# A two-layer diffusion block on one core: modulation pages of four k-tiles, regrouped attention scores, an inverse masked where it is written, and part of the weight lows on GpSimd

## The chip, the core and the metric

The kernel runs on one core of a Trainium2 chip. TensorE multiplies matrices (it loads weights and streams columns; PE and PEld in the profile), VectorE (DVE), ScalarE (ACT) and GpSimd (POOL) do elementwise work, and SyncE (SP) issues the transfers. Every engine works through its own queue in order and waits for others by semaphores. The metric is the device time of one execution in microseconds; three runs of the kernel before took 1391.40, 1393.65 and 1397.22 us, and their median, 1393.65, is the time before.

## The reference

Two layers run over 256 context and 256 latent tokens of 1024 features. Cut to what matters here:

```python
mod = split(silu(c) @ ada_w[layer] + ada_b[layer], 6)        # shift, scale, gate, twice; also for the context
p = modulate(rms_norm(x), mod[0], mod[1]) @ w_in[layer]      # 30 tiles of 128 columns and 16 gate columns
# A: differential attention, 4 heads, two maps each
s = einsum(q, k) * 64 ** -0.5
w = softmax(s[map 0]) - lam * softmax(s[map 1])
o = w @ v
# B: HGRN2 gated recurrence.  C: gated DeltaNet, in chunks of 64:
tri = eye + where(strict, beta * (k @ k.T) * decay, 0)       # inverted for every chunk
u, w = solve(tri, [v * beta, k * beta * exp(gc)])
x = x + mod[2] * rms_norm(concat(A, B, C) @ w_out[layer])
x = x + mod[5] * rms_norm(conv_ffn(modulate(rms_norm(x), mod[3], mod[4])))
```

## The kernel before

The program holds the stream in transposed form, features on partitions and 512 tokens along the columns, and writes its stages as Python generators. `weave` steps several generators in turn at given rates (`RATE`, one row for each layer), which fixes the order in which the program is written; the framework's scheduler then orders the instructions of each engine from that order and the dependencies. The rates stand, in turn, for the projections of attention (`in_proj`), the gated DeltaNet (`gdn`), HGRN2 (`hgrn`), attention (`da`), the modulation (`ada`), and for the DeltaNet beside the late projections.

*Weights.* Each weight tile (`raw`, 128x1024) is split into a rounded part `whi` by ScalarE (L269) and the rest `wlo` by a subtraction (L273), and three matmuls for each k-tile add up the product. `wload` has a number `pool`: so many k-tiles of `wlo`, the last ones, are subtracted on GpSimd and the others on VectorE. In the output projection it is 2, in the attention projections (`proj_copy`) 0.

*Modulation.* `ada` computes one block of 512 columns from four pages of weights. A page holds two k-tiles; the matmul of a k-tile has 32 output rows and goes to one of four groups of array columns (`tile_position`), so a page uses two groups (L317). VectorE copies the result (`adas`, L320), four transposes turn it round (L323), and a reduction adds the four groups (L325). 12 blocks run inside the mixers and 8 in two fills beside the feed-forward part: six in layer 0 (about 400 to 515 us), two in layer 1 (about 1130 to 1190). Eight smaller units at the start (`ada_unit`, L337 and L343) already have four k-tiles to a page, and add the groups by a matmul with the constant `sel`.

*Attention.* For each head, stream and half of 128 queries, `da` makes two score matmuls (`sc`, L1035), one for each map, on different halves of the rows; each gets its maximum (`smx`, L1038), which VectorE multiplies by -0.125 (L1039), and an exponential (`em`, with the scale 0.125) that also sums the row (`ssm`). VectorE scales the first map (L1047) and adds the second (L1048); transposes (`wt`, L1052) and the product with `v` (`do`, L1060) follow.

*Gated DeltaNet.* `gdn` works in two halves of four chunks for two pairs of heads at a time (each list has a page for either pair). GpSimd multiplies the decays in page `gA` with beta (L658), VectorE multiplies them with the products `kk` into `N`, and six levels build the inverse in `MT` (page `gC`). At a level TensorE multiplies `N` with the inverse so far (`rt`), VectorE multiplies with a mask (L704), TensorE multiplies again (`dT`), and VectorE subtracts into `MT` (L707 at the first level, L721 after it). GpSimd also makes `gF` (L727, values times beta) and `gB` (L729, keys times decay), which are used after the inverse. In HGRN2 GpSimd updates `K` at each level (L930).

Of the kernel before, what the change touches and what calls it, by code (L numbers as in the profile page):

```python
# [43 lines left out]
)  # L44
RATE = ((121, 197, 32, 218, 37, 8), (53, 64, 15, 50, 5, 7))

GD_Q, GD_K, GD_V, GD_G = 0, 2, 4, 6
HG_Q, HG_G, HG_F, HG_I = 8, 10, 12, 16
DA_K, DA_V, DA_Q = 18, 22, 26
# [95 lines left out]
class Kernel:  # L145
# [161 lines left out]
    def ada(self, ly, blocks, tags=("raw",), bank="d"):  # L307
        nc = self.nc
        mod = self.mod[ly]
        for j in blocks:  # L310
            ps = self.bank(bank, "ada")
            for kc in range(4):
                w = self.load_raw(self.I["ada_w"][12 * ly + j - 4, kc], 1024, tags[kc % len(tags)]).rearrange("p (k n) -> p k n", k=2)
                for kk in range(2):
                    k = 2 * kc + kk
                    g = k % 4
                    nc.tensor.matmul(ps[32 * g:32 * g + 32, :], self.cs[:, k, :], w[:, kk, :], start=k < 4, stop=k >= 4,  # L317
                                     tile_position=(0, 32 * g))
# [171 lines left out]
    def evac(self, idx, dst, src):  # L490
        if idx % 2:
            self.nc.scalar.copy(dst, src)
        else:
            self.nc.vector.tensor_copy(dst, src)
# [53 lines left out]
    def gdn_gates(self, ly, ab):  # L548
# [48 lines left out]
        nc.vector.scalar_tensor_tensor(be, be, -1.0, beta, ALU.mult, ALU.mult)  # L597
        return dict(la=la, gc=gc, kd=kd, nbe=be, beta=beta)

# [4 lines left out]
    def gdn(self, ly, G, kq, v, last, res):  # L604
# [18 lines left out]
        for hf in range(2):  # L623
# [59 lines left out]
            for lev in range(LEVELS):  # L683
                b = 1 << lev

                def joint(t, c0, c1, bit0):
                    ap = t[:, 256 * bit0 + 64 * c0:256 * bit0 + 64 * c0 + 1]
                    return bass.AP(tensor=ap.tensor, offset=ap.offset,
                                   ap=[list(ap.ap[0]), [2 * b, (c1 - c0) * 32 // b], [b + (256 if bit0 == 0 else -256), 2], [1, b]])

                nb = lambda t: t.rearrange("p (n two b) -> p n two b", two=2, b=b)
                rt = [self.tmp("g2", "rt")[:, 0:256] for hp in HP]
# [18 lines left out]
                for g in range(2):  # L711
# [312 lines left out]
    def da(self, ly, h, q, k, vt, nl, gs, last, res):  # L1024
# [3 lines left out]
        for s, a, b in self.streams(lo):  # L1028
            nk = 2 if s == 0 else 4
            wts = []  # L1030
            for qt in range(2):
                e, rc = [], []
                for m in range(2):
                    ps = self.bank("a", "sc")
                    nc.tensor.matmul(ps[:, :128 * nk], q[64 * m:64 * m + 64, a + 128 * qt:a + 128 * qt + 128],  # L1035
                                     k[64 * m:64 * m + 64, :128 * nk], start=True, stop=True)
# [3 lines left out]
                    em = self.tmp("d2", "em")[:, :128 * nk]  # L1040
                    sm = self.small("sm", 1, 4)
                    self.act(em, ps[:, :128 * nk], AF.Exp, scale=0.125, bias=mx, accum_out=sm)
                    nc.vector.reciprocal(sm, sm)
                    e.append(em)
                    rc.append(sm)
                nc.vector.tensor_tensor(rc[1], rc[1], nl, ALU.mult)
                nc.vector.tensor_scalar(e[0], e[0], rc[0], None, ALU.mult)  # L1047
                nc.vector.scalar_tensor_tensor(e[0], e[1], rc[1], e[0], ALU.mult, ALU.add)  # L1048
                yield
                pt = self.bank("a", "wt")  # L1050
                for kk in range(nk):
                    nc.tensor.transpose(pt[:, 128 * kk:128 * kk + 128], e[0][:, 128 * kk:128 * kk + 128], self.C("ident"))  # L1052
# [313 lines left out]
def pack(inp):  # L1366
    f = lambda a: np.ascontiguousarray(np.asarray(a, dtype=np.float32))
    A = {}
# [15 lines left out]
    for gi, (f0, fn) in enumerate(GROUPS):  # L1384
        A[f"w_down{gi}"] = f(w[:, f0:f0 + fn].transpose(0, 3, 2, 1, 4)).reshape(DEPTH, KT, P, fn * P)
    w = f(inp["ada_w"]).reshape(DEPTH, 4, 2, P, 12, 512)
    A["ada_w"] = f(w.transpose(0, 4, 1, 3, 2, 5)).reshape(DEPTH * 12, 4, P, 1024)[4:]
    w = f(inp["ada_w"])[0].reshape(2, 4, P, 6, KT, P)[:, :, :, :2]
# [42 lines left out]
```

## Time and profile before

| what | us |
|---|---|
| median of three runs | 1393.65 |
| profiled execution, its own time | 1397.04 |
| its span, first to last instruction | 1395.3 |
| TensorE busy (10720 matmuls) | 1298.6 (93%) |
| VectorE busy (1722 instructions) | 892.5 (64%) |
| ScalarE busy (1189) | 658.9 (47%) |
| GpSimd busy (378) | 393.7 (28%) |

The profiled execution is one of its own, beside the three runs. Busy times are sums over the span, so stages with different limits lie in one number; the stages are told apart by stretches of time. In layer 0 the projections and gates end at about 145 us, the mixers at about 400, the output projection at about 455 and the feed-forward part at about 830; in layer 1 the mixers run to about 1145. TensorE's granted clock, 0.974 in the mean, is given for a stretch as a share of 2.4 GHz; 0.5 is the lower level.

### The profile page before, as it was taken

The page shows a single profiled execution, that of the slowest core. Times are in us where ns is not written, and L with a number is a line of the kernel's source. Part 1 is how long each engine was busy: PE and PEld are TensorE (multiplying, and loading weights), DVE is VectorE, ACT ScalarE, POOL GpSimd, SP SyncE. Part 2 cuts the span into 40 slices and gives each one's busy share as a digit, 9 for nine tenths or more (in the row PEclk, how much of TensorE's full clock was granted, in tenths as well). Part 3 has the DMA queues.
Part 4 walks back from the last instruction along what each step waited for, and adds up shares of the span by engine and source line. Part 5 has one row for each costly group of instructions (what it writes and reads, how often), then busy time and mean ns, then how long its engine had stood idle before and what let it go on. Part 6 is the DMA issues. An engine that isn't in the chain of part 4 may idle for free.

```text
span 1395.3 us, 26653 instructions
## 1 busy us (share of the span) xinstructions
PE 1298.6 (93%) x10720; PEld 1048.0 (75%) x10720; DVE 892.5 (64%) x1722; ACT 658.9 (47%) x1189; POOL 393.7 (28%) x378
## 2 busy tenths in 40 slices
PE   5999997999989999999999997999989998999996
PEld 2768665666677678888888886997666765999995
DVE  3565657877647876434543559877697665776665
ACT  3364424444465544323432455675253354655553
POOL 1012014201046223201210266221241024655553
PEclk8999998999999999999999999999999999999998
DMA  8612443112335663323233234544221265455552
GB/s 300 211 46 91 167 165 139 32 47 76 107 121 189 207 217 115 104 92 105 91 101 96 82 122 135 173 145 155 95 103 34 106 243 181 139 183 185 189 167 76
DMA packets 56283, 185.96 MB, mean 133 GB/s; under 512 B 6368, under 2 KB 10464, under 8 KB 56160
## 3 DMA queue, kind: packets, MB, share of 16 engines
q1 hardware_dynamic: 56160, 184.27, 39.9%
q8 instruction: 84, 1.38, 0.4%
q14 instruction: 39, 0.32, 0.1%
HBM read 182.14 MB, written 2.10 MB: 132 GB/s over the span
## 4 chain that ended last, share of the span: by engine, by line
PE 74%; DVE 12%; ACT 5%; POOL 4%; issue 2%; DMA 2%; SPq 0%; DVEq 0%; POOLq 0%; ACTq 0%
PE up L284 8%; PE up L283 8%; PE up L285 8%; PE in L293 6%; PE in L294 5%; PE in L295 5%; PE dn L285 4%; PE dn L284 4%; PE dn L283 4%; PE ada L317 2%; DVE wlo L273 2%; PE sc L1035 2%; PE op L284 1%; PE op L283 1%; PE op L285 1%
## 5 line engine op out<-in xcount | busy, mean ns | idle before, releaser
L273 DVE TENSOR_TENSOR wlo<-raw,whi 128x1024 fp32r<-128x1024 f32 (+2 forms) x241 | 299.8, 1245 | 269.1 <-issue 90.4
L269 ACT CAST whi<-raw 128x1024 fp32r<-128x1024 f32 (+1 forms) x244 | 248.9, 1023 | 122.6 <-PE dn L285 99.0
L285 PE MATMUL up<-h,whi 128*128 128x256 f32 (+1 forms) x768 | 248.7, 324 | 1.3 <-DVE h L441 0.7
L283 PE MATMUL up<-h,whi 128*128 128x256 f32 (+1 forms) x768 | 248.3, 324 | 1.2 <-ACT h L438 1.1
L284 PE MATMUL up<-h,wlo 128*128 128x256 f32 (+1 forms) x768 | 248.0, 324 | 0.9 <-DVE wlo L273 0.9
L293 PE MATMUL in<-h,whi 128*128 128x512 f32 (+1 forms) x496 | 184.8, 373 | 2.2 <-DVE kq L481 2.2
L273 POOL TENSOR_TENSOR wlo<-raw,whi 128x256 fp32r<-128x256 f32 (+1 forms) x111 | 127.1, 1145 | 173.2 <-ACT whi L269 76.4
L294 PE MATMUL in<-h,wlo 128*128 128x512 f32 (+1 forms) x496 | 175.5, 354 | 0.0
L295 PE MATMUL in<-h,whi 128*128 128x512 f32 (+1 forms) x496 | 175.3, 354 | 0.0
L283 PEld LDWEIGHTS up<-h,whi 128*128 128x128 f32 x768 | 145.8, 190 | 19.6 <-issue 4.2
L285 PEld LDWEIGHTS up<-h,whi 128*128 128x128 f32 x768 | 145.9, 190 | 16.4 <-issue 1.7
L284 PEld LDWEIGHTS up<-h,wlo 128*128 128x128 f32 x768 | 145.9, 190 | 15.5 <-DVE wlo L273 1.9
L284 PE MATMUL dn<-gT,wlo 128*128 128x256 f32 (+1 forms) x400 | 127.6, 320 | 3.4 <-DVE wlo L273 3.4
L283 PE MATMUL dn<-gT,whi 128*128 128x256 f32 (+1 forms) x400 | 127.7, 320 | 2.7 <-ACT gT L300 2.7
L285 PE MATMUL dn<-gT,whi 128*128 128x256 f32 (+1 forms) x400 | 127.3, 320 | 0.5 <-POOL gT L302 0.5
L1262 POOL TENSOR_TENSOR u<-u 128x512 f32<-128x512 f32 (+1 forms) x44 | 44.4, 1010 | 278.3 <-DVE u L481 257.5
L293 PEld LDWEIGHTS in<-h,whi 128*128 128x128 f32 x496 | 96.2, 194 | 19.8 <-issue 5.4
L294 PEld LDWEIGHTS in<-h,wlo 128*128 128x128 f32 x496 | 96.2, 194 | 12.7 <-issue 3.5
L295 PEld LDWEIGHTS in<-h,whi 128*128 128x128 f32 x496 | 95.9, 193 | 12.3 <-issue 1.3
L477 ACT ACTIVATE u<-up,vec 128x256 f32<-128x256 f32 (+1 forms) x96 | 61.8, 644 | 75.2 <-PE up L285 75.2
L284 PEld LDWEIGHTS dn<-gT,wlo 128*128 128x128 f32 x400 | 76.7, 192 | 9.1 <-DVE wlo L273 4.0
L283 PEld LDWEIGHTS dn<-gT,whi 128*128 128x128 f32 x400 | 76.8, 192 | 8.2 <-ACT gT L300 3.1
(281 smaller groups left out, 2318.2 us busy)
## 6 DMA issues: line engine op xcount, KB each, us to landing
raw<-ada_w SPq DMA_DIRECT2D x96, 512.0 KB, 4.4
raw<-w_up SPq DMA_DIRECT2D x96, 512.0 KB, 3.5
raw<-w_in SPq DMA_DIRECT2D x68, 512.0 KB, 3.6
raw<-w_down SPq DMA_DIRECT2D x32, 512.0 KB, 3.5
raw<-w_out SPq DMA_DIRECT2D x24, 512.0 KB, 3.5
raw<-w_down SPq DMA_DIRECT2D x24, 384.0 KB, 3.1
x<-xT SPq DMA_DIRECT2D x16, 256.0 KB, 6.1
x_spill<-x SPq DMA_DIRECT2D x8, 128.0 KB, 2.0
```

Source lines behind the costliest of these rows:

```text
L269: nc.scalar.copy(hi[:, :cols], raw[:, :cols])
L273: e.tensor_sub(lo[:, a:b], raw[:, a:b], hi[:, a:b].bitcast(F32))
L283: nc.tensor.matmul(ps, wh[:, k, :], ah, start=first and k == ks[0], stop=False)
L284: nc.tensor.matmul(ps, wl[:, k, :], ah, start=False, stop=False)
L285: nc.tensor.matmul(ps, wh[:, k, :], al, start=False, stop=last and k == ks[-1])
L293: nc.tensor.matmul(ps, wh[:, k, :], ah, start=k == 0, stop=False)
L294: nc.tensor.matmul(ps, wl[:, k, :], ah, start=False, stop=False)
L295: nc.tensor.matmul(ps, wh[:, k, :], al, start=False, stop=k == n - 1)
L317: nc.tensor.matmul(ps[32 * g:32 * g + 32, :], self.cs[:, k, :], w[:, kk, :], start=k < 4, stop=k >= 4, tile_position=(0, 32 * g))
L477: nc.scalar.activation(dst, ps, AF.Identity, scale=w3[1], bias=bias)
L1035: nc.tensor.matmul(ps[:, :128 * nk], q[64 * m:64 * m + 64, a + 128 * qt:a + 128 * qt + 128], k[64 * m:64 * m + 64, :128 * nk], start=True, ...
L1262: self.nc.gpsimd.tensor_mul(us[0][:, lo:], us[0][:, lo:], us[1][:, lo:])
```

## The change

`ada` takes four k-tiles of 256 columns from a page, so that each page uses all four groups, and adds the groups by four matmuls with `sel` in place of transposes and reduction; the weights are packed in that order. In `da` both score matmuls of a query half are written next to each other, the second map's first; the maximum is negated in its own instruction, the scale 0.125 moves to the copy of the query projection (ScalarE), the scaling of the first map moves from VectorE to ScalarE, and lambda goes in by a `tensor_scalar`. In `gdn` the sign moves into beta (`nb`), `rt` is no longer masked but copied by ScalarE, and the new `fill` writes only the masked places of `MT` by `copy_predicated`. `proj_copy` gives two k-tiles of the lows to GpSimd. Four of six rates change in each layer.

```diff
-RATE = ((121, 197, 32, 218, 37, 8), (53, 64, 15, 50, 5, 7))
+RATE = ((121, 179, 35, 218, 38, 8), (47, 64, 10, 62, 5, 6))
...
-            for kc in range(4):
-                w = self.load_raw(self.I["ada_w"][12 * ly + j - 4, kc], 1024, tags[kc % len(tags)]).rearrange("p (k n) -> p k n", k=2)
-                for kk in range(2):
-                    k = 2 * kc + kk
-                    g = k % 4
-                    nc.tensor.matmul(ps[32 * g:32 * g + 32, :], self.cs[:, k, :], w[:, kk, :], start=k < 4, stop=k >= 4,
-                                     tile_position=(0, 32 * g))
+            prev = []
+            for i in range(4):
+                half, kc = i // 2, i % 2
+                w = self.load_raw(self.I["ada_w"][12 * ly + j - 4, i], 1024, tags[i % len(tags)]).rearrange("p (k n) -> p k n", k=4)
+                for g in range(4):
+                    x = nc.tensor.matmul(ps[32 * g:32 * g + 32, 256 * half:256 * half + 256], self.cs[:, 4 * kc + g, :], w[:, g, :],
+                                         start=kc == 0, stop=kc == 1, tile_position=(0, 32 * g))
+                    prev = [self._dep(x, prev)]
...
-                nc.tensor.transpose(ps2[:, 128 * i:128 * i + 128], st[:, i * 128:(i + 1) * 128], self.C("ident"))
-            sm = self.small("adr", 8)
-            nc.vector.reduce_sum(sm, ps2.rearrange("p (a g s) -> p a s g", a=4, g=4)[:, :, 0:2, :], axis=AX.X)
+                nc.tensor.matmul(ps2[:, 2 * i:2 * i + 2], st[:, 128 * i:128 * i + 128], self.C("sel"), start=True, stop=True)
...
-        w = self.wload(self.I["w_in"][ly, idx], 8, 128)
+        w = self.wload(self.I["w_in"][ly, idx], 8, 128, 2)
...
-        self.evac(idx, dst[:, lo:], ps[:, lo:])
+        self.evac(idx, dst[:, lo:], ps[:, lo:], 0.125 if idx >= DA_Q else None)
...
-                nc.gpsimd.tensor_tensor(ck(X[hp]), ck(X[hp]), b64(hp, "beta"), ALU.mult)
+                nc.gpsimd.tensor_tensor(ck(X[hp]), ck(X[hp]), b64(hp, "nb"), ALU.mult)
...
+                def fill(t, src):
...
+                    nc.vector.copy_predicated(out, m.bitcast(U32), v(src))
...
-                for hp in HP:
-                    nc.vector.tensor_tensor(ck(rt[hp]), ck(src[hp]), hgm[:, lev, :].unsqueeze(1).to_broadcast([P, 4, 64]), ALU.mult)
                 if lev == 0:
                     for hp in HP:
-                        nc.vector.tensor_tensor(joint(MT[hp], 0, 4, 0), joint(MT[hp], 0, 4, 0), nb(rt[hp]), ALU.subtract)
+                        fill(MT[hp], src[hp])
                     yield
                     continue
+                for hp in HP:
+                    nc.scalar.copy(rt[hp], src[hp])
...
-                    nc.vector.tensor_tensor(joint(MT[hp], 0, 4, 0), joint(MT[hp], 0, 4, 0), nb(ps2[hp][:, 0:256]), ALU.subtract)
+                    fill(MT[hp], ps2[hp][:, 0:256])
...
-                    mx = self.small("mx", 1, 4)
-                    nc.vector.reduce_max(mx, ps[:, :128 * nk], axis=AX.X)
-                    nc.vector.tensor_scalar(mx, mx, -0.125, None, ALU.mult)
...
-                    self.act(em, ps[:, :128 * nk], AF.Exp, scale=0.125, bias=mx, accum_out=sm)
...
-                nc.vector.tensor_scalar(e[0], e[0], rc[0], None, ALU.mult)
...
+                    for n, t in enumerate(qs):
+                        for m in (1, 0):
+                            x = nc.tensor.matmul(ps[m][:, 128 * nk * n:128 * nk * n + 128 * nk],
...
+                            prev.append(self._dep(x, prev[-1:]))
...
+                        nc.vector.reduce_max(mx[m][:, :len(qs)], ps[m][:, :128 * nk], axis=AX.X, negate=True)
...
+                nc.scalar.activation(e0, e0, AF.Copy, scale=r0)
+                nc.vector.reciprocal(r1, r1)
+                nc.vector.tensor_scalar(r1, r1, nl, None, ALU.mult)
+                nc.vector.scalar_tensor_tensor(e0, e1, r1, e0, ALU.mult, ALU.add)
```

The first place is GpSimd's queue in layer 0, where the DeltaNet's second half begins, in the kernel before (`sgl` is a small copy, `gA_1983` and `gA_1984` are the pages of the two pairs of heads, `sbeta` is beta, `skd` the decays):

```order
L678 COPY sgl_2153<-gB_1986 128x8
L658 TENSOR_TENSOR gA_1983<-gA_1983,sbeta_640 128x512
L727 TENSOR_TENSOR gF_2725<-gB_1985,sbeta_640 128x512
L729 TENSOR_TENSOR gB_1985<-gB_1985,skd_676 128x256
L727 TENSOR_TENSOR gF_2725<-gB_1986,sbeta_640 128x512
L729 TENSOR_TENSOR gB_1985<-gB_1985,skd_676 128x256
L729 TENSOR_TENSOR gB_1986<-gB_1986,skd_676 128x256 x2
L658 TENSOR_TENSOR gA_1984<-gA_1984,sbeta_640 128x512
L930 TENSOR_TENSOR K_203_1175<-K_203_1175,F_202_1174 128x128x2x2 x2
```

The same place in the changed kernel (`snbt` is beta with the sign turned, `wlo` with L273 is a weight tile's lows):

```order
L681 COPY sgl_2309<-gB_2072 128x8
L661 TENSOR_TENSOR gA_2069<-gA_2069,snbt_683 128x512
L661 TENSOR_TENSOR gA_2070<-gA_2070,snbt_683 128x512
L738 TENSOR_TENSOR gF_2868<-gB_2071,sbeta_640 128x512
L740 TENSOR_TENSOR gB_2071<-gB_2071,skd_676 128x256 x2
L273 TENSOR_TENSOR wlo_2338<-raw_2335,whi_2337 128x256
L738 TENSOR_TENSOR gF_2868<-gB_2072,sbeta_640 128x512
L740 TENSOR_TENSOR gB_2072<-gB_2072,skd_676 128x256 x2
L273 TENSOR_TENSOR wlo_2605<-raw_2602,whi_2604 128x256
```

The second `gA` page's multiplication moved from behind all of `gF` and `gB` to right behind the first, and the lows of weight tiles stand between the two pairs' `gF` and `gB` and behind them.

The second place is the same one in layer 1, in the kernel before:

```order
L678 COPY sgl_10110<-gB_9932 128x8
L658 TENSOR_TENSOR gA_9929<-gA_9929,sbeta_8652 128x512
L727 TENSOR_TENSOR gF_10684<-gB_9931,sbeta_8652 128x512
L658 TENSOR_TENSOR gA_9930<-gA_9930,sbeta_8652 128x512
L729 TENSOR_TENSOR gB_9931<-gB_9931,skd_8688 128x256 x2
L727 TENSOR_TENSOR gF_10684<-gB_9932,sbeta_8652 128x512
L729 TENSOR_TENSOR gB_9932<-gB_9932,skd_8688 128x256 x2
```

And in the changed kernel:

```order
L681 COPY sgl_10182<-gB_9981 128x8
L661 TENSOR_TENSOR gA_9978<-gA_9978,snbt_8747 128x512
L738 TENSOR_TENSOR gF_10635<-gB_9980,sbeta_8704 128x512
L740 TENSOR_TENSOR gB_9980<-gB_9980,skd_8740 128x256 x2
L661 TENSOR_TENSOR gA_9979<-gA_9979,snbt_8747 128x512
L738 TENSOR_TENSOR gF_10635<-gB_9981,sbeta_8704 128x512
L740 TENSOR_TENSOR gB_9981<-gB_9981,skd_8740 128x256 x2
```

Here the second `gA` page's multiplication moved the other way, past the two `gB` multiplications of the first pair.

## Rows read from the trace of the kernel before

**Rows 1.** Stretches: length, busy of PE, PEld, DVE, ACT, POOL (count), clock, DMA.
```profile
215.00:400.00 185.00, 164.06 (x1918) 115.83 (x1916) 130.68 (x343) 86.11 (x216) 39.19 (x37) 0.93 0.21 70
445.00:515.00 70.00, 65.13 (x426) 46.12 (x425) 53.87 (x98) 34.78 (x62) 17.19 (x18) 1.00 0.65 218
985.00:1145.00 160.00, 147.12 (x1823) 104.28 (x1821) 121.48 (x330) 70.81 (x159) 35.86 (x31) 0.97 0.33 117
```

**Rows 2.** Waits of TensorE, 215 to 400: who for whom, sum us, times, longest.
```profile
PE rt L602 <- DVE gC L707: 8.3, 1, 8.3
PE wt L1052 <- DVE em L1048: 5.0, 6, 1.3
```

**Rows 3.** GpSimd in order of time, 213 to 231: start, us, instruction.
```profile
214.56 1.05 POOL L658 TENSOR_TENSOR gA<-gA,sbeta 128x512 f32<-128x512 f32 x1 [2.13 <-ACT gA L222]
215.56 3.70 POOL L727 TENSOR_TENSOR gF<-gB,sbeta 128x512 f32<-128x512 f32 x1
219.34 2.63 POOL L729 TENSOR_TENSOR gB<-gB,skd 128x256 f32<-128x256 f32 x1
...
225.75 1.04 POOL L658 TENSOR_TENSOR gA<-gA,sbeta 128x512 f32<-128x512 f32 x1
226.75 3.18 POOL L930 TENSOR_TENSOR K<-K,F 128x512 f32<-128x512 f32 x2
```

**Rows 4.** ScalarE, VectorE and TensorE in order of time around the 8.3 us.
```profile
217.55 0.63 ACT L222 ACTIVATE gA<-gA 128x512 f32<-128x512 f32 x1
...
226.82 1.72 DVE L668 TENSOR_TENSOR gA<-gA 128x256 f32<-128x256 f32 x1 [3.18 <-POOL gA L658]
...
233.47 0.87 PE L602 MATMUL rt<-gC,gA 64*64 64x64 f32 x10 [8.32 <-DVE gC L707]
```

**Rows 5.** Short stretches behind the stall and in layer 1, columns as above.
```profile
226.00:236.00 10.00, 2.53 (x35) 2.00 (x35) 7.67 (x21) 4.54 (x11) 3.85 (x3) 0.70 0.29 107
236.00:246.00 10.00, 10.00 (x111) 7.01 (x109) 6.88 (x23) 5.29 (x12) 0.00 (x0) 0.62 0.18 54
...
1030.00:1040.00 10.00, 7.22 (x118) 4.93 (x119) 10.00 (x24) 4.50 (x11) 5.86 (x6) 0.95 0.38 141
```

**Rows 6.** The modulation's products (L317) alone, by stretch.
```profile
145.00:215.00 70.00, 9.62 (x80) 2.09 (x80) 1.00 0.53 188
445.00:515.00 70.00, 19.02 (x72) 2.67 (x72) 1.00 0.65 218
```

**Rows 7.** The start's products and weight loads of `sel`; weight loads of the transposes.
```profile
40.38 0.64 PE L337 MATMUL ada<-raw,cs 128*32 128x256 f32 x8
...
48.08 0.62 PEld L343 LDWEIGHTS ada<-consts,adas 128*128 128x128 f32 x4
...
484.76 0.46 PEld L323 LDWEIGHTS ada<-consts,adas 128*128 128x128 f32 x4
```

**Rows 8.** Score matmuls in order of time: one alone, a pair side by side.
```profile
247.48 1.12 PE L1035 MATMUL sc<-qk 64*128 64x512 f32 x2
...
295.80 1.13 PE L1035 MATMUL sc<-qk 64*128 64x512 f32 x4
```

**Rows 9.** Durations by line: busy us, mean ns, idle; last two 215 to 400.
```profile
L704 DVE TENSOR_TENSOR rt<-rt,consts 128x256 f32<-128x256 f32 x40 | 15.1, 410 | 6.2 <-PE rt L602 6.2
...
L917 DVE COPY_PREDICATED Stot<-consts,hs 128x512 f32<-128x512 uint32 x12 | 8.1, 730 | 1.6 <-PE hs L892 1.6
...
L1047 DVE TENSOR_SCALAR em<-em,ssm 128x256 f32<-128x256 f32 (+1 forms) x16 | 6.6, 413 | 0.2
...
L1039 DVE TENSOR_SCALAR smx<-smx 128x1 f32<-128x1 f32 x32 | 4.6, 145 | 0.4
```

**Rows 10.** A weight tile's lows on both engines, output projection, in order of time.
```profile
408.17 0.96 DVE L273 TENSOR_TENSOR wlo<-raw,whi 128x768 fp32r<-128x768 f32 x1 [1.92 <-PE op L285]
408.20 1.53 POOL L273 TENSOR_TENSOR wlo<-raw,whi 128x256 fp32r<-128x256 f32 x1 [0.65 <-PE op L285]
409.04 0.97 DVE L404 TENSOR_TENSOR acc<-acc,sq 128x256 f32<-128x256 f32 x1
```

More of the change, by code (lines that the diff above doesn't have):

```diff
@@ L483, in proj_copy, with evac @@
     def proj_copy(self, ly, idx, hT, lo, dst):
-        w = self.wload(self.I["w_in"][ly, idx], 8, 128)
+        w = self.wload(self.I["w_in"][ly, idx], 8, 128, 2)
         ps = self.bank("d", "in")
         yield from self.dense_gen(ps[:, lo:], w, hT, lo, NTOK)
-        self.evac(idx, dst[:, lo:], ps[:, lo:])
+        self.evac(idx, dst[:, lo:], ps[:, lo:], 0.125 if idx >= DA_Q else None)
         yield
-    def evac(self, idx, dst, src):
-        if idx % 2:
+    def evac(self, idx, dst, src, scale=None):
+        if scale is not None:
+            self.nc.scalar.activation(dst, src, AF.Copy, scale=scale)
+        elif idx % 2:
             self.nc.scalar.copy(dst, src)
@@ L597, in gdn_gates @@
         nc.vector.scalar_tensor_tensor(be, be, -1.0, beta, ALU.mult, ALU.mult)
-        return dict(la=la, gc=gc, kd=kd, nbe=be, beta=beta)
+        nbeta = self.small("nbt", 32, 1)
+        nc.vector.tensor_scalar(nbeta, beta, -1.0, None, ALU.mult)
+        return dict(nb=nbeta, la=la, gc=gc, kd=kd, nbe=be, beta=beta)
     def quad(self, items):
@@ L689, in joint @@
                                    ap=[list(ap.ap[0]), [2 * b, (c1 - c0) * 32 // b], [b + (256 if bit0 == 0 else -256), 2], [1, b]])
+                def fill(t, src):
+                    ap = t[:, 0:1]
+                    out = bass.AP(tensor=ap.tensor, offset=ap.offset,
+                                  ap=[list(ap.ap[0]), [64, 4], [2 * b, 32 // b], [b + 256, 2], [1, b]])
+                    v = lambda t: t.rearrange("p (c n two b) -> p c n two b", c=4, two=2, b=b)
+                    m = hgm[:, lev, :].rearrange("p (n two b) -> p n two b", two=2, b=b).unsqueeze(1).to_broadcast([P, 4, 32 // b, 2, b])
+                    nc.vector.copy_predicated(out, m.bitcast(U32), v(src))
                 nb = lambda t: t.rearrange("p (n two b) -> p n two b", two=2, b=b)
@@ L1031, in da @@
             for qt in range(2):
[L1032 to L1036, printed above, removed]
-                    mx = self.small("mx", 1, 4)
-                    nc.vector.reduce_max(mx, ps[:, :128 * nk], axis=AX.X)
-                    nc.vector.tensor_scalar(mx, mx, -0.125, None, ALU.mult)
-                    em = self.tmp("d2", "em")[:, :128 * nk]
-                    sm = self.small("sm", 1, 4)
-                    self.act(em, ps[:, :128 * nk], AF.Exp, scale=0.125, bias=mx, accum_out=sm)
-                    nc.vector.reciprocal(sm, sm)
-                    e.append(em)
-                    rc.append(sm)
@@ L1046, in da @@
-                nc.vector.tensor_tensor(rc[1], rc[1], nl, ALU.mult)
-                nc.vector.tensor_scalar(e[0], e[0], rc[0], None, ALU.mult)
-                nc.vector.scalar_tensor_tensor(e[0], e[1], rc[1], e[0], ALU.mult, ALU.add)
+                if True:
+                    qs = (qt,)
+                    ps = [self.bank("a", "sc") for m in range(2)]
+                    prev = []
+                    for n, t in enumerate(qs):
+                        for m in (1, 0):
+                            x = nc.tensor.matmul(ps[m][:, 128 * nk * n:128 * nk * n + 128 * nk],
+                                                 q[64 * m:64 * m + 64, a + 128 * t:a + 128 * t + 128],
+                                                 k[64 * m:64 * m + 64, :128 * nk], start=True, stop=True)
+                            prev.append(self._dep(x, prev[-1:]))
+                    mx = [self.small("mx", 2, 4) for m in range(2)]
+                    es = {}
+                    for m in range(2):
+                        nc.vector.reduce_max(mx[m][:, :len(qs)], ps[m][:, :128 * nk], axis=AX.X, negate=True)
+                        for n, t in enumerate(qs):
+                            em = self.tmp("d2", "em")[:, :128 * nk]
+                            sm = self.small("sm", 1, 8)
+                            self.act(em, ps[m][:, 128 * nk * n:128 * nk * n + 128 * nk], AF.Exp, bias=mx[m][:, n:n + 1], accum_out=sm)
+                            es[t, m] = em, sm
@@ L1049, in da @@
+                (e0, r0), (e1, r1) = es[qt, 0], es[qt, 1]
+                nc.vector.reciprocal(r0, r0)
+                nc.scalar.activation(e0, e0, AF.Copy, scale=r0)
+                nc.vector.reciprocal(r1, r1)
+                nc.vector.tensor_scalar(r1, r1, nl, None, ALU.mult)
+                nc.vector.scalar_tensor_tensor(e0, e1, r1, e0, ALU.mult, ALU.add)
                 yield
@@ L1051, in da @@
                 for kk in range(nk):
-                    nc.tensor.transpose(pt[:, 128 * kk:128 * kk + 128], e[0][:, 128 * kk:128 * kk + 128], self.C("ident"))
+                    nc.tensor.transpose(pt[:, 128 * kk:128 * kk + 128], e0[:, 128 * kk:128 * kk + 128], self.C("ident"))
                 wt = self.tmp("r2", "wt")
@@ L1385, in pack @@
         A[f"w_down{gi}"] = f(w[:, f0:f0 + fn].transpose(0, 3, 2, 1, 4)).reshape(DEPTH, KT, P, fn * P)
-    w = f(inp["ada_w"]).reshape(DEPTH, 4, 2, P, 12, 512)
-    A["ada_w"] = f(w.transpose(0, 4, 1, 3, 2, 5)).reshape(DEPTH * 12, 4, P, 1024)[4:]
+    w = f(inp["ada_w"]).reshape(DEPTH, 2, 4, P, 12, 2, 256)
+    A["ada_w"] = f(w.transpose(0, 4, 5, 1, 3, 2, 6)).reshape(DEPTH * 12, 4, P, 1024)[4:]
     w = f(inp["ada_w"])[0].reshape(2, 4, P, 6, KT, P)[:, :, :, :2]
```

2 lines of the change are left out of this document (1 added, 1 removed).

## The prediction

> **What bounds the kernel now.** I read four views in this order: busy time by stretch, TensorE's waits, the order of time around the longest wait, and durations by line. The stretches [rows 1] show a kernel that lives on TensorE: even in the two mixer stretches (215 to 400 us in layer 0, 985 to 1145 in layer 1) it is busy 164.06 of 185 and 147.12 of 160 us. So only two things can shorten the run: less work on TensorE, or less of its idle time, which is 20.9 us in the first stretch and 12.9 in the second. The waits [rows 2] name what is in the first: one wait of 8.3 us (`rt` on VectorE's `gC`, L707) and six of 5.0 us in sum (`wt` on `em`, L1048). The order of time shows what lies behind the 8.3 us: GpSimd [rows 3] multiplies the first `gA` page at 214.56, then takes six multiplications for `gF` and `gB`, and comes to the second `gA` only at 225.75, although ScalarE had that page's exponential done at 218.2 [rows 4]. VectorE sits 3.18 us for it, needs until 234 for the inverse's first level, and TensorE starts `rt` at 233.47. Then the clock pays again [rows 5]: in 226 to 236 the granted clock is 0.70, in 236 to 246 it is 0.62, so of these 20 us some 6.0 and 7.6 are at the 1.2 GHz level.
>
> The sum is made against the profiled execution's own 1397.04 us (span 1395.3, 1.7 around it), which is 3.4 us above the median of 1393.65; at the end I take 3.4 off.
>
> **A. Modulation pages.** Four pages per block stay four, with transfers of the same number and size; each now brings four k-tiles of 256 columns instead of two of 512. Where pages come one by one, a page costs TensorE 19.02 / 18 = 1.06 us today (72 records, four a page, 445 to 515) [rows 6]; the new form exists in the kernel's start (L337) and takes 0.64 us a page [rows 7]. There are 32 such pages in the two fills; I count 24 as coming alone: 24 x 0.42 = -10 us. Where all four pages wait ready (12 blocks inside the mixers) a block costs 9.62 / 5 = 1.92 us today and between that and 4 x 0.64 = 2.56 in the new form; the columns streamed are the same, so I stay near today's row with 2.1, +2 us. The second step gets dearer: four transposes load weights for 0.46 us, while the form with `sel` loads for 0.62 us per two products, since an fp32 product passes twice [rows 7]. Four products are 1.24 at most, so +0.78 a block at most and, as runs follow each other closely, I take +0.65; 20 blocks, +13 us, 8 of them in the mixers and 5 in the fills. On the path: the mixers get +10 of work, of which TensorE's idle slots hide a little, +9. The fills get 5 less, but there the elementwise chain of the norms sets much of the pace (TensorE is busy 65.13 of 70), so -3. A is +6, bounds -3 (the fills' 5 whole and a little more, the mixers' part hidden) and +17 (2.56 and 0.78 a block in the mixers, nothing from the fills).
>
> **B. Scores.** Two score matmuls of one head use different halves of the rows, and a pair side by side takes 1.13 us where one alone takes 1.12 [rows 8]. But 19 of the 24 pairs stand side by side in TensorE's queue already, and in the changed order it is 17. The pairing does not do what its name says; what is left is that the first one issued now waits for the bank that comes free last, so that staggered pairs close up. -1, bounds -4 and +3.
>
> **C. GpSimd's queue in layer 0.** The rates move the gated delta net against the rest, and the second `gA` multiplication now stands right behind the first, ahead of all of `gF` and `gB`. Its page is ready at 218.2, so it could end at 219.3 instead of 226.8: 7.5 us. TensorE has about the same work between `kk` and `rt` as before, a little less, so I take 6.5 of the 8.3. The slow clock behind the stall costs half of what TensorE did at 1.2 GHz (some 2 and 7.6 us): -4.5. C is -11, bounds 0 and -13.
>
> **D. VectorE gets lighter.** Gone are 48 mask products (0.41 each, 19.7 us) and 24 scalings of `e0` (0.413 mean, 9.9 us); the 48 tiny multiplications by -0.125 (0.145 each) overlap their neighbours, I count half, 3.5 us [rows 9]. `copy_predicated` takes the place of a subtraction of the same size: 0.73 us at 512 columns, so about 0.41 at 256; nothing. That is 33 us, about a tenth of VectorE's load in the mixers (130.68 and 121.48 us in the two stretches [rows 1], the rest ahead of them); 20 small sums of the modulation and four copies of `q` go too, uncounted. Where it is full and TensorE waits (10.00 of 10 us at 1030 to 1040, TensorE at 7.22 [rows 5]) a tenth comes back directly. The idle time left after C is 20.9 + 12.9 - 8.3 = 25.5 us; a third of it, -8, with the clock that goes with it. Against it: the scaling of `e0` moves behind the second exponential on ScalarE, one hop more in 24 chains that end in `wt`; behind a scaling that waits stand ScalarE's casts of the next weights, which are a tile ahead of TensorE. At 0.4 to 0.5 us each that is +12 at worst; the negated maximum saves a hop in the same chains, so I take +1. The 40 copies of `rt` that ScalarE takes over stand in the place of VectorE's products in the same chain; ScalarE is busy 86 of 185 and 71 of 160 us [rows 1], and they hide. D is -7, bounds -25 and +12.
>
> **E. Lows on GpSimd.** 28 weight tiles give their last two k-tiles to GpSimd, VectorE's part shrinks by a quarter. In the output projection, which does it today, the pair reads [rows 10]: VectorE 0.96 us from 408.17, GpSimd 1.53 us from 408.20, so it ends at 409.73, and the next VectorE instruction, a 128x256 sum, takes 0.97. GpSimd first waits for VectorE's part and then VectorE for GpSimd's. The long L668 beside GpSimd's `K` (1.72 us from 226.82) [rows 3, 4] is the same. Per tile VectorE saves at most 0.96 x 256 / 768 = 0.32 us, and loses at most 0.97 - 0.41 = 0.56 (a sum of that size takes 0.41 undisturbed, as L704 does [rows 9]): -9 to +7 over 28 tiles, and I take 0. TensorE uses the two k-tiles last, so GpSimd has most of a tile's time for them; nothing is added there.
>
> The Trainium skill, "SBUF — State Buffer", section "Who interferes with whom", says that VectorE with two SBUF inputs and GpSimd reading SBUF exclude each other for a whole instruction, which speaks against E. The 0.97 us row agrees. If every low on GpSimd locked VectorE for its own 0.57 us (1.53 - 0.96) it would be 28 x 0.57 = 16 us on VectorE's side, half of what D takes off it, and the run would be some 4 us longer than forecast.
>
> **F. GpSimd in layer 1.** Here the new order puts the second `gA` behind one `gF` and two `gB`; before, only behind one `gF`. +1, upper bound 13 (a stall like the one in layer 0, 8.3 + 4.5).
>
> **Sum.** 6 - 1 - 11 - 7 + 0 + 1 = -12, so 1385 in the profiled execution's terms and, less 3.4, 1381 on the scale of the median.
>
> **Rivals.** *Nothing gained:* the relief of VectorE does not reach TensorE because its queue is in order and the next wait ends last, and C brings half (-5): 6 - 1 - 5 + 0 + 1 = +1, some 1395. For it: beside the 8.3 us the idle time is in waits of one or two microseconds, of which each can be replaced by another. Against it: VectorE really is full where TensorE waits. *More gained:* the idle time left falls by 70% (-18, so D is -17) and A's fill part comes through whole (A is +4): 4 - 1 - 11 - 17 + 0 + 1 = -24, about 1370. For it: where VectorE is full, TensorE waits for nothing else. Against it: only 30 to 40 us of the mixers look like that. *Slower: the stall moves to layer 1.* The second `gA` of layer 1 waits behind `gF` and both `gB`; at layer 0's durations (3.70 and 2.63 us with VectorE beside them [rows 3]) that is over 7 us, and as in layer 0 the chain to `rt` behind it takes 6.7 more (226.8 to 233.5) while TensorE has a few microseconds of projection. Price 8.3 + 4.5 = +13, and with VectorE held by GpSimd there, D falls to -1; with A's mixer part whole and nothing from the fills (+10): 10 - 1 - 11 - 1 + 0 + 13 = +10, about 1404. It decides when that second multiplication starts more than 5 us after the first. Against it: it is the shorter queue of the two, three instructions against six in layer 0 today.
>
> **Chances.** Forecast 0.50 (its own range 1375 to 1389), more gained 0.14, nothing gained 0.20, slower 0.16. A measurement of this kernel tells about 0.5% (7 us) from no change. Below 1386.7 lie nine tenths of the forecast and all of "more": 0.60; the rest of the forecast, "nothing" and a little of "slower" (0.02): 0.26; slower 0.14. The range of 8 in 10 reaches from 1366, below "more", to 1400, past "nothing gained" and short of "slower".
>
> **What would show it.** C right: no wait of `rt` over 3 us in layer 0's second half of the delta net, clock 1.00 behind it. A right: the modulation's products in 445 to 515 fall to about 12 us, the second step rises from 0.46 to about 1.1 us of weight loads a block. B right: score pairs at 1.13 us, but no fewer separate ones. D right: VectorE's busy time falls by some 35 us, and TensorE's idle time in the mixers by 15 to 20. E right: 28 more GpSimd lows of over 1 us, and VectorE's parts near 1 us. The prediction is wrong if the wait in C is still there or comes up in layer 1, or if waits of `in` for lows on GpSimd appear.

## The result: slower by 0.8%, outside the range

The changed kernel took 1406.47 us in the median (1400.82 to 1413.38, 12 runs), the kernel before 1395.83 beside it; the ratio is 1.0075 with an interval of 1.0054 to 1.0095. The forecast was 1381, the range ended at 1400. The profiled execution, 1400.94 us with a span of 1399.2, is one of the shortest of the twelve, so the profile shows only some 4 of the 10.6 us. The rest goes with the clock: the mean granted clock of the twelve runs goes from 0.974 (1400.94 us) down to 0.962 (1413.38 us), with a median of 0.969, while the runs of the kernel before beside the experiments have medians of 0.977 to 0.979.

### The profile page after: what moved, and what is told of

The parts are those of the page before. It is cut to its first block, busy times and chain, and to the rows that moved or that the text cites. A ratio compares the mean times of both kernels' runs of the same rounds, so it can differ in the third digit from the quotient of the medians.

```text
span 1399.2 us, 27455 instructions
## 1 busy us (share of the span) xinstructions
PE 1307.8 (93%) x11120; PEld 1071.9 (77%) x11120; DVE 869.0 (62%) x1580; ACT 682.6 (49%) x1257; POOL 421.5 (30%) x406
## 4 chain that ended last, share of the span: by engine, by line
PE 53%; DVE 9%; ACT 2%; issue 1%; POOL 1%; DMA 1%; DVEq 0%; POOLq 0%; ACTq 0%
PE up L284 8%; PE up L285 8%; PE up L283 8%; PE dn L285 4%; PE dn L284 4%; PE dn L283 4%; PE in L293 3%; PE in L295 2%; PE in L294 2%; DVE wlo L273 2%; PE ada L317 1%; DVE x L467 1%; PE ada L324 1%; PE ss L382 1%; PE sc L1049 1%
## 5 line engine op out<-in xcount | busy, mean ns | idle before, releaser
L273 DVE TENSOR_TENSOR wlo<-raw,whi 128x768 fp32r<-128x768 f32 (+2 forms) x241 | 296.4, 1231 | 263.4 <-PE up L284 91.2
L273 POOL TENSOR_TENSOR wlo<-raw,whi 128x256 fp32r<-128x256 f32 (+1 forms) x139 | 153.3, 1106 | 277.2 <-ACT whi L269 128.4
L1281 POOL TENSOR_TENSOR u<-u 128x512 f32<-128x512 f32 (+1 forms) x44 | 49.0, 1114 | 284.9 <-DVE u L480 284.9
```

What stands on the lines that cost most here:

```text
L273: e.tensor_sub(lo[:, a:b], raw[:, a:b], hi[:, a:b].bitcast(F32))
L1281: self.nc.gpsimd.tensor_mul(us[0][:, lo:], us[0][:, lo:], us[1][:, lo:])
```

## The profile after

The stretches of [rows 1], now (length, busy of PE, PEld, DVE, ACT, POOL, clock, DMA):

```profile
215.00:400.00 185.00, 176.04 (x2010) 128.91 (x2009) 122.12 (x285) 107.64 (x265) 47.46 (x52) 0.98 0.26 82
445.00:515.00 70.00, 64.94 (x528) 55.23 (x527) 49.94 (x83) 34.24 (x57) 16.59 (x17) 0.93 0.66 217
985.00:1145.00 160.00, 143.91 (x1764) 103.55 (x1763) 112.05 (x271) 72.24 (x165) 42.28 (x39) 0.94 0.33 112
```

Layer 0 went the way of the forecast: TensorE is busy for 176.04 of 185 us instead of 164.06, VectorE's time falls from 130.68 to 122.12. The third row goes the other way: TensorE's idle time there is 16.1 us where it was 12.9, at a clock of 0.94, although VectorE has 9.4 us less to do. In the second row the clock, 1.00 before, is 0.93.

TensorE's longest waits between 215 and 400, in answer to [rows 2], then GpSimd around the second half of the DeltaNet, in layer 0 and in layer 1, in answer to [rows 3]:

```profile
PE wt L1071 <- DVE em L1067: 3.5, 4, 1.7
PE sc L1049 <- DVE rope L1031: 1.3, 1, 1.3
```

```profile
219.21 2.14 POOL L661 TENSOR_TENSOR gA<-gA,snbt 128x512 f32<-128x512 f32 x2
226.07 1.04 POOL L738 TENSOR_TENSOR gF<-gB,sbeta 128x512 f32<-128x512 f32 x1 [4.73 <-ACT gB L545]
...
1014.22 1.04 POOL L661 TENSOR_TENSOR gA<-gA,snbt 128x512 f32<-128x512 f32 x1 [1.06 <-ACT gA L222]
1015.22 1.22 POOL L738 TENSOR_TENSOR gF<-gB,sbeta 128x512 f32<-128x512 f32 x1
1016.52 1.43 POOL L740 TENSOR_TENSOR gB<-gB,skd 128x256 f32<-128x256 f32 x2
1019.31 1.09 POOL L661 TENSOR_TENSOR gA<-gA,snbt 128x512 f32<-128x512 f32 x1 [1.36 <-ACT gA L222]
```

The 8.3 us wait is gone, and in layer 0 both `gA` pages are multiplied one right behind the other. In layer 1 the second page starts 5.1 us after the first, just past the point that the rival set; yet the longest wait of `rt` there is 2.1 us, and the next rows tell where the time is instead. They are two stretches of layer 1: from the first `rt` to the last (the DeltaNet's inverses), and from there to the first `up` matmul (the tail: late projections, HGRN and attention, the output projection, two modulation blocks). The kernel before:

```profile
950.30:1069.50 119.20, 108.05 (x1357) 76.61 (x1360) 95.02 (x228) 54.30 (x113) 28.98 (x24) 0.96 0.30 102
1069.50:1179.30 109.80, 102.66 (x1172) 76.57 (x1162) 68.71 (x183) 52.32 (x115) 26.73 (x24) 1.00 0.46 159
```

The changed kernel:

```profile
945.10:1061.00 115.90, 101.10 (x1295) 73.66 (x1291) 84.95 (x172) 56.09 (x124) 34.28 (x29) 0.94 0.29 96
1061.00:1188.60 127.60, 120.25 (x1358) 89.49 (x1348) 73.95 (x185) 59.63 (x132) 34.48 (x32) 0.96 0.43 150
```

The inverses gain 3.3 us, the tail loses 17.8. TensorE's idle time in the tail is 7.1 us before and 7.4 now: what grew there is its busy time, at a clock of 0.96 for 1.00. HGRN's products `hs` tell what moved: here in the changed kernel, and behind it in experiment e1, where layer 1 has its old rates (count, durations in ns, first and last start):

```profile
L903 PE MATMUL hs<-Q,kj x192: 218/218/284, 1017.0 to 1118.9; 64*64 64x64 f32 x192
```

```profile
L903 PE MATMUL hs<-Q,kj x192: 218/218/366, 986.6 to 1069.2; 64*64 64x64 f32 x192
```

## The experiments

Ratios are to the kernel before on the same chip; an interval is about 0.002 to either side, so the difference of two ratios is good to some 0.003, 4 us. "New" and "old" order are the rates of a layer as in the changed kernel and as before.

| run | order L0, L1 | work | us | ratio (interval) |
|---|---|---|---|---|
| changed | new, new | all new | 1406.47 | 1.0075 (1.0054, 1.0095) |
| e1 | new, old | all new | 1387.87 | 0.9953 (0.9930, 0.9975) |
| e5 | old, old | all new | 1401.44 | 1.0057 (1.0038, 1.0075) |
| e6 | old, new | old | 1414.07 | 1.0134 (1.0106, 1.0162) |
| e11 | new, old | old | 1387.99 | 0.9961 (0.9946, 0.9976) |
| e9 | new, HGRN 10 | all new | 1398.35 | 1.0035 (1.0016, 1.0054) |
| e10 | new, attention 62 | all new | 1388.97 | 0.9972 (0.9954, 0.9989) |
| e16 | new, HGRN 20 | all new | 1398.66 | 1.0022 (1.0003, 1.0041) |
| e2 | new, new | old modulation | 1404.50 | 1.0054 (1.0033, 1.0075) |
| e3 | new, new | old DeltaNet | 1397.75 | 1.0005 (0.9984, 1.0027) |
| e4 | new, new | old lows | 1404.20 | 1.0063 (1.0039, 1.0087) |
| e7 | new, old | old DeltaNet | 1388.86 | 0.9950 (0.9936, 0.9965) |
| e8 | new, old | old modulation | 1387.61 | 0.9952 (0.9935, 0.9968) |
| e12 | new, old | old attention | 1400.16 | 1.0053 (1.0040, 1.0066) |
| e13 | new, old | old lows | 1389.52 | 0.9954 (0.9934, 0.9975) |
| e14 | new, old | new attention alone | 1385.00 | 0.9920 (0.9899, 0.9941) |
| e15 | new, old | new lows alone | 1396.43 | 1.0012 (0.9997, 1.0027) |
| e17 | new, old | e14 and pages, transposes | 1385.68 | 0.9931 (0.9907, 0.9955) |
| e18 | new, old | e14 and new modulation | 1385.20 | 0.9931 (0.9906, 0.9956) |

### The order of layer 1: e1, e6, e9, e10, e16

```diff
 e1:  -(47, 64, 10, 62, 5, 6)   +(53, 64, 15, 50, 5, 7)   on the changed kernel
 e6:  -(53, 64, 15, 50, 5, 7)   +(47, 64, 10, 62, 5, 6)   on the kernel before
 e9:  e1 with (53, 64, 10, 50, 5, 7)
 e10: e1 with (53, 64, 15, 62, 5, 7)
 e16: e1 with (53, 64, 20, 50, 5, 7)
```

> The changed kernel with the four rates of layer 1 put back to (53, 64, 15, 50, 5, 7); layer 0 keeps the new rates. In the changed kernel the stretch from the first rt of layer 1 to the feed-forward part there is 14.5 us longer (950.3 to 1179.3 before, 945.1 to 1188.6 after), while layer 0 up to the feed-forward part is 8.7 us shorter. Theory 1 (the order of layer 1, set by its rates, is what costs): the time falls by 8 to 14 us against the changed kernel, to 1392 to 1398, at or a little under the kernel before. Theory 2 (the work that changed, modulation or DeltaNet, is what costs, wherever it stands): it falls by under 3 us, to 1403 to 1406.

> The kernel before with only the rates of layer 1 changed to (47, 64, 10, 62, 5, 6). Theory 1 (the order itself is what costs): slower than the kernel before by 10 to 19 us, 1406 to 1415. Theory 2 (the order costs only together with the new DeltaNet or modulation work): within 5 us of it, 1391 to 1401.

Theory 1 holds in both, with more than it gave e1: the four rates cost 17 us with the new work (1.0075 to 0.9953) and 19 with the old (e6). The new work is not needed for it.

> The changed kernel whose layer 1 has the old rates but for HGRN's (10 in place of 15). With all four old it took 1387.87, with all four new 1406.47. Theory H (HGRN's recurrence, at the lower rate, runs on after the DeltaNet and its chain ends the mixers: hs last at 1118.9 in the changed kernel, at 1069.2 with the old rates): 1400 to 1408. Theory A (the attention, at the higher rate, is what collides): within 4 us of 1388.

> The changed kernel whose layer 1 has the old rates but for attention's (62 in place of 50). Theory A: 1396 to 1407. Theory H: within 4 us of 1388. If neither this nor the run with HGRN's rate alone moves by over 5 us, the cost lies in the two slower rates of the projections (47 and 6) or only in the rates together.

> The changed kernel with the old rates in layer 1 but for HGRN's, which goes the other way (20 in place of 15). Theory H (what runs beside the DeltaNet's inverse is free, what is left for the tail behind it costs): as the tail behind it had little of HGRN already, within 4 us of 1388. Theory 2 (the lower the rate the more it costs, in proportion; 5 lower cost 10.5 us): 1376 to 1381.

HGRN's rate alone costs 11 of the 17 us (theory H, a little under its range), attention's 3, which is within the error. And HGRN's rate moved the other way costs 10, which neither theory had. The two slower rates of the projections were not tried alone. The two stretches of layer 1 in e1, where HGRN has 15:

```profile
941.40:1059.90 118.50, 108.78 (x1421) 78.55 (x1424) 85.37 (x193) 62.26 (x137) 36.01 (x34) 0.97 0.32 104
1059.90:1173.70 113.80, 106.78 (x1264) 82.94 (x1253) 65.12 (x164) 55.55 (x121) 29.60 (x27) 0.96 0.50 159
```

Against these rows the changed kernel's inverses are only 2.6 us shorter, though TensorE has 7.7 us less to do in them, and its tail is 13.8 us longer, with 13.5 us more for TensorE. Not only HGRN moved there. TensorE's part of the projections (`in`), then of `hs`, in the tail of e1:

```profile
1059.90:1173.70 113.80, 23.04 (x102) 0.96 0.50 159
1059.90:1173.70 113.80, 1.39 (x64) 0.96 0.50 159
```

And in the changed kernel's tail, in the same order:

```profile
1061.00:1188.60 127.60, 29.09 (x120) 0.96 0.43 150
1061.00:1188.60 127.60, 4.08 (x128) 0.96 0.43 150
```

The stretches of e9, with 10 for HGRN, and the place of `hs`:

```profile
946.60:1064.90 118.30, 108.42 (x1357) 78.59 (x1356) 80.39 (x181) 61.08 (x133) 33.48 (x30) 0.96 0.31 104
1064.90:1187.30 122.40, 113.91 (x1332) 85.87 (x1324) 70.03 (x176) 57.03 (x125) 34.68 (x31) 0.94 0.46 152
```

```profile
L903 PE MATMUL hs<-Q,kj x192: 218/219/367, 1030.0 to 1120.2; 64*64 64x64 f32 x192
```

In e16, with 20:

```profile
943.90:1071.80 127.90, 110.98 (x1485) 81.47 (x1484) 91.33 (x205) 62.66 (x138) 37.95 (x35) 0.96 0.29 96
1071.80:1186.70 114.90, 106.47 (x1191) 83.14 (x1181) 61.69 (x152) 54.82 (x120) 28.55 (x26) 0.94 0.46 153
```

At 10 the inverses take as long as at 15 (118.3 and 118.5 us), though part of HGRN has left them, and the tail is 8.6 us longer. At 20 the tail is no shorter (114.9 and 113.8) and the inverses need 9.4 us more. Of the three values 15 is the best; none between them was tried.

The two losses are not alike. TensorE's idle time in both stretches together is 16.7 us at 15, 18.4 at 10 and 25.4 at 20, and its busy time 215.6, 222.3 and 217.4. So at 20 it is idle time that came on top, at 10 busy time for the same work. Part of that is the clock, which at 10 is lower by 0.01 and 0.02; from these rows the estimate is 4 of the 6.8 us (the share of time at the lower level is twice what the clock lacks to 1.00, and half of that time is lost). These profiled executions lie 0.4 (e1), 2.1 (e9) and 5.7 us (e16) above the medians, so the rows of e16 show the loss too large.

### The order of layer 0: e5, e11

```diff
 e5:  both rows of RATE as before, on the changed kernel
 e11: -(121, 197, 32, 218, 37, 8)   +(121, 179, 35, 218, 38, 8)   on the kernel before
```

> The changed kernel with both layers' rates as before, so that only the work differs from the kernel before. With layer 1 alone put back the time was 1387.87. Theory 1 (layer 0's new order is the gain that the prediction put into C, the GpSimd queue): the stall before rt comes back in layer 0 and the time rises by 7 to 13 us, to 1395 to 1401. Theory 2 (the gain in layer 0 is VectorE's lighter load, D): it stays within 3 us of 1388.

> The kernel before with only the rates of layer 0 changed. Theory 1 (the parts add up: new order of layer 0 -13.6, new order of layer 1 +18.6, new work +5.8): 1380 to 1385, faster than any kernel so far. Theory 2 (the new order of layer 0 gains only with the new work, whose GpSimd and VectorE load is another): 1390 to 1398.

Three of the six rates differ in layer 0: the DeltaNet's, HGRN's and the modulation's. With the new work its order brings 14 us (1.0057 to 0.9953), just past the upper end of theory 1; with the old work 5 (e11), between the two theories. In the profiles the first `op` matmul of layer 0 comes 9.2 us earlier with the new work (392.9 to 383.7, e5 and e1) and 10.8 with the old (392.2 to 381.4, before and e11), so with the old work half of it is lost again behind the mixers.

The same runs weigh the work as a whole: with the order as before it costs 8 us (e5), with layer 0's new order it is worth 1 (0.9953 in e1, 0.9961 in e11), which is no difference.

GpSimd's queue is not all that the stall hangs on. In e5 the second `gA` stands behind `gF` and `gB` as before, but these run faster, and it is done 9.1 us after the first began (212.48 to 221.62) instead of 12.2 [rows 3]; TensorE's wait is there all the same. Its row, then rows of GpSimd, VectorE and ScalarE:

```profile
PE rt L605 <- DVE ssm L1066: 7.7, 1, 7.7
```

```profile
220.58 1.04 POOL L661 TENSOR_TENSOR gA<-gA,snbt 128x512 f32<-128x512 f32 x1
225.14 3.18 POOL L941 TENSOR_TENSOR K<-K,F 128x512 f32<-128x512 f32 x2 [3.52 <-DVE F L890]
...
221.34 2.28 DVE L939 TENSOR_TENSOR Q<-Q,F 128x1024 f32<-128x1024 f32 x1
...
223.80 1.19 DVE L890 TENSOR_TENSOR F<-F 128x1024 f32<-128x1024 f32 x1
...
225.52 1.42 DVE L671 TENSOR_TENSOR gA<-gA 128x256 f32<-128x256 f32 x1
...
229.59 0.16 DVE L1063 RECIPROCAL ssm<-ssm 128x1 f32<-128x1 f32 x1 [1.06 <-ACT em L222]
...
230.38 1.24 DVE L700 COPY_PREDICATED gC<-consts,gC 128x256 f32<-128x256 uint32 x1
231.25 0.38 DVE L1066 TENSOR_SCALAR ssm<-ssm,nlam 128x1 f32<-128x1 f32 x1
...
228.35 0.62 ACT L922 COPY kj<-K 128x512 f32<-128x512 f32 x1 [8.91 <-POOL K L941]
228.99 0.47 ACT L222 ACTIVATE em<-sc,smx 128x256 f32<-128x256 f32 x1
```

VectorE takes the page (L671) only 3.9 us after it is there, without a wait: it is behind in its own queue, with HGRN's `Q` and `F` (3.5 us) ahead. ScalarE stands 8.91 us for HGRN's `K` on GpSimd before it can copy `kj`; behind that copy stand the exponentials, and VectorE loses 1.06 us to them (L1063) before it goes on to the inverse. The wait's row names L1066, but that ends at the same time as the first masked write of the inverse (L700, 230.38 + 1.24 = 231.62), and it is the page of this write that `rt` reads. So most of this wait is VectorE's queue with HGRN's update in it, and about 1 us came through ScalarE. In the kernel before, where `Q`, `F` and `K` stood at the same place, VectorE did wait for the page, 3.18 us [rows 4], so the lateness of the page had at most that much of the 8.3. The new rates move HGRN's update as a whole: in the changed kernel `Q`, `F` and `K` start at 205.2, 207.4 and 208.8, ahead of this place, in e11 at 204.4, 206.9 and 208.2, and the longest wait of `rt` in e11 between 215 and 400 is 0.8 us. No run changes HGRN's rate of layer 0 alone.

### The parts of the work, one undone at a time: e2, e3, e4, e7, e8, e12, e13

```diff
 e2, e8:  the hunk of ada and the packing of ada_w as before
 e3, e7:  the hunks of gdn as before (nb, fill, the copy of rt)
 e4, e13: -wload(self.I["w_in"][ly, idx], 8, 128, 2)   +wload(self.I["w_in"][ly, idx], 8, 128)
 e12:     the hunk of da and evac's scale as before
```

In the changed kernel's order:

> The changed kernel with the modulation as before: pages of two k-tiles, transposes and reduction, and the weights packed for it (two small buffers are a few bytes narrower to make room). Theory 1 (order of layer 1): within 3 us of the changed kernel, 1403 to 1409. Theory 2a (the modulation costs, by the products with sel and by shorter matmuls that break up the others; the prediction's +6, or up to +17): the time falls by 6 to 12 us, to 1394 to 1400.

> The changed kernel with the DeltaNet's inverse as before: rt masked by VectorE, subtraction into MT, no copy of rt on ScalarE and no copy_predicated. Theory 1: VectorE gets 48 products back, so the time stays or rises by up to 4 us, 1406 to 1410. Theory 2b (the masked write is dearer than a subtraction: the eight of the first level took 1.30 us each instead of 0.66 and 0.44, and the copy of rt is a hop on ScalarE): the time falls by 4 to 10 us, to 1396 to 1402.

> The changed kernel with the lows of the attention projections whole on VectorE again (28 tiles). Theory 1: within 3 us, 1403 to 1409. Theory 2c (28 more subtractions on GpSimd hold up VectorE where it is full, as at 1029 us, where a VectorE part of 768 columns took 2.28 us with GpSimd beside it): the time falls by 4 to 8 us, to 1398 to 1402.

Modulation and lows lie within the error (-3 and -2 us); the old DeltaNet is 10 us faster there, as theory 2b said. With layer 1's old rates that is gone:

> As the run with layer 1's rates put back (1387.87), and the DeltaNet's inverse as before too. With the new order of layer 1 the old DeltaNet was worth 8.7 us. Theory 1 (it helped there only because VectorE and the clock were in trouble in that order): 1385 to 1392. Theory 2 (the masked write and the copy of rt on ScalarE cost by themselves): the time falls by 5 to 10 us, to 1378 to 1383. Theory 3 (the prediction's D: VectorE's 23 us of products matter): it rises by 3 to 7 us, to 1391 to 1395.

> As the run with layer 1's rates put back (1387.87), and the modulation as before too. Theory 1 (the prediction's A, +6 for the change): 1380 to 1384. Theory 2 (the trace of the changed kernel: products 8.8 us less, second step 7.1 us more, so -2): 1387 to 1392.

> As the run with layer 1's rates put back (1387.87, ratio 0.9953), and the lows of the attention projections whole on VectorE. Theory 1 (the lows on GpSimd are the part that costs what the attention gains): 1375 to 1382. Theory 2 (the prediction's E, no gain and no loss): 1384 to 1391.

> As the run with layer 1's rates put back (1387.87), and the attention as before too (scores, maxima and scalings; the scale of the exponential). The DeltaNet and the modulation put back there were worth +1 and 0. Theory 1 (the attention's hop over ScalarE costs; the new work costs 5.8 us in sum and none of the other two does): 1381 to 1385. Theory 2 (the lighter VectorE gains, the prediction's D): 1390 to 1395.

Undone alone, three parts are worth nothing in this order (0 us each, within the error), so theory 1 of e7 holds, and the price of e3 appears only in the changed kernel's order. The attention is worth 14 us, the way of the prediction's D and more than theory 2 gave it.

### One part alone, and the fastest kernel: e14, e15, e17, e18

```diff
 e14: e11 and the hunks of da and evac
 e15: e11 and wload(..., 8, 128, 2) in proj_copy
 e17: e14 and the pages of ada; transposes, reduce_sum as before
 e18: e14 and the whole hunk of ada
```

> The kernel before with layer 0's new rates (ratio 0.9961, some 1388), and of the work only the attention changed. Theory 1 (the attention gains some 13 us by itself, as undoing it cost 12 to 14): 1373 to 1379. Theory 2 (it gains only where the other parts have loaded VectorE, ScalarE and GpSimd; the parts don't add up): 1383 to 1390.

> The kernel before with layer 0's new rates (some 1388), and of the work only the lows of the attention projections on GpSimd. Theory 1 (they cost): 1394 to 1402. Theory 2 (nothing): 1385 to 1391.

> The kernel before with layer 0's new rates and the new attention (ratio 0.9920, 1385.0), and pages of four k-tiles, but still transposes and reduction behind them. Theory 1 (TensorE's time counts: products 8.8 us less in the trace, of which the mixers hide some): 1377 to 1382. Theory 2 (as for the whole modulation, nothing reaches the end): 1383 to 1388.

> As the run with pages alone, and the products with sel in place of transposes and reduction. Theory 1: 7 us over the run with pages alone (second step 7.1 us more), 1384 to 1389. Theory 2: within 3 us of it, 1382 to 1388.

The attention alone gains 6 us on e11 (theory 2) and makes the fastest kernel: 1385.0 us, 0.8% under the kernel before; e17 and e18 lie within the error of it. The lows alone cost 7 (theory 1), though undoing them in e13 changed nothing; the parts do not add up. The modulation adds nothing either way. Where its gain goes is to be seen in 425 to 515 us, the fill of layer 0. First e14, then e17:

```profile
425.00:515.00 90.00, 83.69 (x567) 63.48 (x564) 68.15 (x116) 47.55 (x83) 28.19 (x28) 1.00 0.67 216
```

```profile
425.00:515.00 90.00, 78.22 (x632) 65.56 (x621) 64.75 (x113) 46.26 (x82) 27.64 (x27) 0.92 0.66 213
```

TensorE has 5.5 us less to do in the same stretch, but the fill is not faster: its products start between 424.1 and 495.8 us in e14, between 424.6 and 498.1 in e17. The saved time is idle time, and the clock is 0.92 instead of 1.00. In the 13 profiles with the new pages the clock is 0.91 to 0.98 here, in the 7 with the old pages 0.96 to 1.00. It is low with the `sel` products too (0.91 in e18), where TensorE is busy for 82.3 us; what paces the fill, and why the clock is lower, no run separates.

## Why the prediction was wrong

**The step that failed is F.** "Here the new order puts the second `gA` behind one `gF` and two `gB` ... +1, upper bound 13." It took the order of layer 1 for a matter of GpSimd's queue at one place. Measured, that order costs 17 us, and 19 with the old work, beyond its bound. What the rates changed is where HGRN and the projections run, and no term of the sum had that: a rate going from 15 to 10 was read for its effect on one queue, not for the work that it takes out of the inverses' stretch and puts behind it. HGRN's rate alone is 11 of the 17 us (e9); that the projections' rates are the rest is likely from the tail's rows, but not shown.

F is the larger part of the miss, not all of it. On the way from the kernel before by e5 and e1 to the changed one the work is +8 where A, B, D and E had -2, layer 0's order -14 where C had -11, layer 1's order +17 where F had +1.

**The slower rival had the time (1404) but not the mechanism.** Its condition came true (5.1 us), its stall did not: `rt` waits 2.1 us.

**C was right in sign and near in size, and half right in cause.** -11 forecast; -14 with the new work, -5 with the old. The wait is gone, but C took 6.5 us from GpSimd's queue where its own row had VectorE wait 3.18 for the page. In e5 the page comes 3 us sooner after the first one and the wait stays at 7.7 us; HGRN's update in VectorE's queue holds it as well. That the whole order came so near to C is in part luck.

**A was 6 us too dear, within its bounds.** Forecast +6, measured 0 (e8, e18). The sizes in the profile, before and after:

```profile
L317 PE MATMUL ada<-raw,cs 128*32 128x512 f32 x320 | 54.8, 610 | 5.0 <-DMA raw<-ada_w 5.0
L323 PE MATMUL ada<-consts,adas 128*128 128x128 f32 x80 | 13.5, 295 | 5.4 <-DVE adas L320 5.4
```

```profile
L317 PE MATMUL ada<-raw,cs 128*32 128x256 f32 x640 | 47.2, 396 | 2.4 <-DMA raw<-ada_w 2.1 <-ACT raw L493 0.3
L324 PE MATMUL ada<-consts,adas 128*128 128x2 f32 x160 | 21.1, 254 | 9.3 <-DVE adas L321 9.2
```

The products fall by 7.6 us (forecast -8); the second step rises by 7.6, where the sum had +13, priced by the weight loads of [rows 7].

**B and D.** B cannot be told from D's part in the attention; together they are -6 (e14) to -14 (e12), against -1 and -7. The rest of D is nothing: the DeltaNet's products, the larger share of VectorE's relief, are worth 0 with layer 1 in its old order (e7). D's sign was some 35 us less of VectorE; it fell by 23.5 (892.5 to 869.0), and TensorE's idle time fell by 12.0 us in the first mixer stretch and rose by 3.2 in the second. VectorE had 95 us of work in the 119 of layer 1's inverses before and 85 in e1, and they took 119.2 and 118.5. One price was low: the masked write of the first level takes 1.30 us each (10.4 / 8) where I had 0.41 [rows 9]:

```profile
L700 DVE COPY_PREDICATED gC<-consts,dT 128x256 f32<-128x256 uint32 x40 | 18.0, 502 | 22.3 <-PE dT L605 22.1
L700 DVE COPY_PREDICATED gC<-consts,gC 128x256 f32<-128x256 uint32 x8 | 10.4, 1487 | 0.0
```

**E was right beside the other changes and at its upper bound alone.** 0 forecast, 0 in e13, +7 in e15. The Trainium skill ("SBUF — State Buffer", section "Who interferes with whom") has a VectorE instruction with two SBUF inputs contend with a GpSimd instruction that reads SBUF, which would make a loss of this sign; no run here separates it from a shift of the order.

**What stays open:** why the DeltaNet's new form costs 10 us in the changed kernel's order, and why the lows cost alone. (In e15's profile the first `up` of layer 0 comes as in e11, 444.8 and 445.0 us; 3 of the 7 us arise in the feed-forward part of that layer, which has none of these lows, and 3 in layer 1's inverses.) Each part also shifts the order of its neighbours, and no run holds the order fixed while the work changes.

## What to carry to other kernels

Where a table of rates sets the order, read first what each rate moves out of a stretch with a long chain and into one that is full: a stretch that gets little shorter when work leaves it carries that work for nothing up to a point, and here both sides of that point cost (inverses of 118.5 us at 15 and 127.9 at 20, a tail 8.6 us longer at 10). Test the rates of each layer apart from the work, since here the orders decided 14 and 17 us, and the work as a whole cost 8 us in one order and nothing in the other. A part's worth in one order says little of its worth in another.

## What was not expected of the hardware

Work taken off TensorE in the fill of layer 0 did not come back as time but went with a lower granted clock (0.92 in e17 for 1.00 in e14, 425 to 515 us). And a `copy_predicated` of 128x256 took 0.45 us in the median at the inverse's later levels, but 1.2 us or more at the first, where the places that it writes are single columns (b = 1). At the first level it also reads its source from SBUF and not from PSUM; no run separates the two.
